# The down projection by seven products of quarters, token-major, for the first two parts of each FFN, and gate/up product blocks that share a PSUM bank

## The chip, the core and the metric

The kernel runs on one core of a Trainium2 chip. The metric is device time in microseconds of one execution. The core has TensorE (matmuls; PE in the profile, with the load of the stationary operand as a row of its own, PEld), VectorE (DVE), ScalarE (ACT), GpSimd (POOL) and SyncE (SP), which run side by side and wait for each other by semaphores. Matmuls accumulate in PSUM, which has banks of 512 float32 columns per partition; all else lies in SBUF.

## The reference

A decoder trunk of two layers (`DEPTH`) on 512 tokens and 1024 features, float32. Each layer runs a SwiGLU FFN, a mixer, a cross attention and a second FFN, so there are four FFNs, all of one form:

```
def swiglu_ffn(h, w_gu, w_down):
    gu = h @ w_gu
    gate, up = jnp.split(gu, 2, axis=-1)
    return (jax.nn.silu(gate) * up) @ w_down
...
f = swiglu_ffn(rms_norm(h, ffn1_pre_g[i]), ffn1_w_gu[i], ffn1_w_down[i])
h = h + 0.5 * rms_norm(f, ffn1_post_g[i])
```

`D_FF` is 2816, which is 22 blocks of 128 hidden features. Mixers and cross attention are the same in both kernels.

## The kernel before

Every float32 product is made from three matmuls in a reduced format: an operand is split into `hi` (a cast on ScalarE) and `lo` (the remainder, a subtraction on VectorE), and `mm3` (L77 to L81) adds hi·hi, hi·lo and lo·hi into PSUM. So each weight tile and each activation tile passes once through ScalarE (L74) and once through VectorE (L75) before TensorE can use it. `parts` does that for a raw weight tile of 512 KB, into a ring of four `whi`/`wlo` pairs (`N_W`); the raw tiles have a ring of seven (`N_R`).

An FFN works through the 22 hidden blocks in three parts of 8, 8 and 6 (`FF_PARTS`, L33). In a part it first makes the hidden features, two blocks at a time, feature-major (features on partitions, tokens along a row), by `seven` (L292): gate and up of the two blocks by seven products of quarters in place of eight, a scheme of the Strassen kind. The activations' quarters and their sums (`x.a11`, `x.a12`, `x.a22`, `x.x1` to `x.x4`) are made once per FFN in `Quarters`; the weights' sums are made from the quarters `b11`, `b21`, `b22` and the sums `t1`, `t3`, partly by DMAs that add into a raw tile (L299 and L302, on the GpSimd queue). A product is 2 x 4 x 3 = 24 matmuls with 256 columns, so a `seven` has 168. PSUM accumulators A, B and C are two banks each, one for each of the two feature blocks u, with 256 of 512 columns in use. The first two blocks of an FFN are made without the scheme (`fm_quad`). `done` applies silu and the gate product and splits the result into the `Hidden` tile of the part.

Then the part's down projection: for each half c of the 1024 output columns, four accumulators (`accs`, one for each 128 tokens), over 8 hidden blocks, `tm_part` (L334): hidden features are stationary, weights move 512 columns at a time, so 2 x 8 x 4 x 3 = 192 matmuls with 512 columns. The result is copied to `f` (ScalarE, first part) or added to it (VectorE, second part). The third part's projection is joined with the norm that follows (`tm_last`).

Which instruction comes first on an engine is decided when the kernel is built: a scheduler with a cost model of its own lays out one fixed list for each engine, and an engine works through its list in order. The SBUF pool `big` has 13 tiles of 8 KB per partition (`N_S`).

Of the kernel before, what the change touches and what calls it, by code (L numbers as in the profile page):

```python
# [4 lines left out]
F32 = mybir.dt.float32  # L5
# [30 lines left out]
def trunk_kernel(tc, x, mem, ffn1_pre_g, ffn1_w_gu, ffn1_w_down, ffn1_post_g,  # L36
# [8 lines left out]
    with ExitStack() as es:  # L45
# [194 lines left out]
        def fm_raw(w, i, c0):  # L240
            raw = raw_tile([P, 4, 256])
            nc.sync.dma_start(out=raw, in_=fm_rows(w, i, c0))
            return raw
# [26 lines left out]
        def psa():  # L270
            return pa.tile([P, 512], F32, name="psa", tag="a")
# [20 lines left out]
        def seven(w, ca, cb, x, done, mid=None):  # L292

            b21 = fm_raw(w, 1, ca)
            b11 = fm_raw(w, 0, ca)
            t1 = fm_raw(w, 0, cb)
            nc.gpsimd.dma_start(out=t1, in_=fm_rows(w, 0, ca), accum_op=ALU.add)  # L299
            b22 = fm_raw(w, 1, cb)  # L300
            t3 = fm_raw(w, 0, cb)
            nc.gpsimd.dma_start(out=t3, in_=fm_rows(w, 1, cb), accum_op=ALU.add)  # L302
            banks = {n: [psa(), psa()] for n in "BAC"}
            out_a = qt([P, 2, SEQ])
            out_b = qt([P, 2, SEQ])
            lo_h, hi_h = slice(0, HALF), slice(HALF, SEQ)

            def product(n, raw, ops, start):
                wh = parts(raw, (P, 4, 256))
                for u in range(2):  # L310
                    for k in range(4):
                        mm3(banks[n][u][:, :HALF], tuple(t_[:, k, u * P:(u + 1) * P] for t_ in wh),
                            (ops[:, 0, k], ops[:, 1, k]), start and k == 0, k == 3, False)
                return [b[:, :HALF] for b in banks[n]]

            pb = product("B", b21, x.a12, True)
            for u, p_ in enumerate(product("A", b11, x.a11, True)):
                nc.scalar.copy(out=out_a[:, u, lo_h], in_=p_)
                nc.vector.tensor_tensor(out=out_a[:, u, lo_h], in0=pb[u], in1=out_a[:, u, lo_h], op=ALU.add)
            for u, p_ in enumerate(product("C", t1, x.x1, True)):  # L320
                nc.scalar.copy(out=out_b[:, u, hi_h], in_=p_)
            nc.vector.tensor_tensor(out=t1, in0=t1, in1=b22, op=ALU.add)
            for u, p_ in enumerate(product("A", t1, x.x2, False)):
                nc.scalar.copy(out=out_b[:, u, lo_h], in_=p_)
            for u, p_ in enumerate(product("C", b22, x.x4, False)):
                nc.vector.tensor_tensor(out=out_b[:, u, lo_h], in0=p_, in1=out_b[:, u, lo_h], op=ALU.subtract)
            for u, p_ in enumerate(product("A", t3, x.x3, False)):
                nc.vector.tensor_tensor(out=out_b[:, u, hi_h], in0=out_b[:, u, hi_h], in1=p_, op=ALU.subtract)
            if mid:
                mid()  # L330
            nc.vector.tensor_tensor(out=t1, in0=t1, in1=b21, op=ALU.add)
            done(out_a, out_b, product("A", t1, x.a22, False))

        def tm_part(accs, a, w, ks, first, last, ts=range(NT)):  # L334
            for k in ks:
# [128 lines left out]
                return t[:, 0, j % 2, c0:c1], t[:, 1, j % 2, c0:c1]  # L464

        def ffn(pre, w_gu, w_down, post_g, nxt):
            f = None
            for j0, j1 in FF_PARTS:
                hid = Hidden()
                for j in range(j0, j1, 2):  # L470
                    if j == 0:
                        ws = pre.ws
                        ps = fm_quad([ws[0], ws[2], ws[1], ws[3]], pre, True)
                        s_ = qt([P, 2, SEQ])
                        for i in range(2):
                            nc.scalar.activation(out=s_[:, i, :], in_=ps[2 * i], func=AF.Silu)
                            nc.vector.tensor_tensor(out=s_[:, i, :], in0=ps[2 * i + 1], in1=s_[:, i, :],
                                                    op=ALU.mult)
                        ht = hid.put(j - j0)
                        split(ht[:, 0], ht[:, 1], s_)  # L480
                        continue

                    def done(ga, ub, last, j=j):
                        nc.scalar.activation(out=ga[:, :, :HALF], in_=ga[:, :, :HALF], func=AF.Silu)
                        for u in range(2):
                            nc.scalar.activation(out=ga[:, u, HALF:], in_=last[u], func=AF.Silu)
                        nc.vector.tensor_tensor(out=ga, in0=ga, in1=ub, op=ALU.mult)  # L487
                        ht = hid.put(j - j0)
                        split(ht[:, 0], ht[:, 1], ga)

                    wk = {}
                    mid = (lambda: last_weights(w_down, j0, j1 - j0, wk, True)) if j == NFF - 2 else None
                    seven(w_gu, j * P, FF + j * P, pre.x, done, mid)
                n = j1 - j0
                if j1 == NFF:
                    nx = nxt()
                    last_weights(w_down, j0, n, wk, False)
                    tm_last(hid, wk, n, post_g, nx, f)
                    break
                fresh = f is None  # L500
                if fresh:
                    f = [big(F32, (P, 2, D)) for _ in range(2)]
                for c in range(2):
                    accs = [psa() for _ in range(NT)]
                    for k0 in range(0, n, 4):
                        wk = dict(zip(range(k0, k0 + 4), w_tm(w_down, j0 + k0, 4, c * 512)))
                        tm_part(accs, hid, wk, range(k0, k0 + 4), 0, n - 1)
                    for t in range(NT):
                        dst = f[t // 2][:, t % 2, c * 512:(c + 1) * 512]
                        if fresh:  # L510
                            nc.scalar.copy(out=dst, in_=accs[t])
                        else:
                            nc.vector.tensor_tensor(out=dst, in0=accs[t], in1=dst, op=ALU.add)
            return nx

        spilled = {}
# [439 lines left out]
```

## Time and profile before

| | |
|---|---|
| median of three runs | 2040.62 us (2039.35 to 2043.59) |
| the profiled execution | 2044.45 us, of which its span is 2042.6 us |
| TensorE busy | 1992.6 us, 98% of the span |
| VectorE / ScalarE / GpSimd busy | 1329.9 / 991.9 / 176.3 us |
| mean granted clock of TensorE | 0.994 |
| moved by DMA | 277.96 MB |

The span reaches from the first to the last instruction of one execution; times below are microseconds from its start. In the timeline of TensorE a row's second number is the duration of one matmul, and since matmuls overlap in the array, the cost of one is the distance from its start to the next one's. A bracket at a row's end is the idle time of the engine ahead of it and what ended it.

### The profile page before, as it was taken

What the parts mean: (1) busy time and instruction counts of PE and PEld (TensorE: products, weight loads), DVE (VectorE), ACT (ScalarE), POOL (GpSimd) and SP (SyncE); (2) the same over time, 40 slices, a digit from 0 to 9 for tenths busy, and PEclk for the clock granted to TensorE, in tenths of its full rate; (3) what the DMA queues carried; (4) which work ended last, traced back from release to release, by engine and by line L of the source; (5) the groups of instructions that cost most, each with busy time, mean ns of one, the idle gap of its engine ahead of it and who ended that gap; (6) DMA issues with size and microseconds to landing.
All of it is one profiled execution on the core that took longest, in us unless ns stands there. A gap on an engine that the chain in (4) does not pass through costs nothing. (4 is left out here: it accounts for less than half of the span.)

```text
span 2042.6 us, 31836 instructions
## 1 busy us (share of the span) xinstructions
PE 1992.6 (98%) x13033; PEld 1826.1 (89%) x13033; DVE 1329.9 (65%) x1743; ACT 991.9 (49%) x1565; POOL 176.3 (9%) x181
## 2 busy tenths in 40 slices
PE   7999999998999999999999999999999999999998
PEld 7989999887878879899898989999878879999897
DVE  6737567799946458457487836657666648647475
ACT  6535345544555356445255635435545545445262
POOL 1001010121010011010001101010000000000000
PEclk9999999999999999999999999999999999999999
DMA  6747554324632235565572656646152225657561
GB/s 197 197 113 190 158 137 146 115 83 133 232 130 93 61 94 143 156 143 168 125 215 53 160 149 148 182 115 196 63 175 78 78 57 139 177 124 176 130 158 54
DMA packets 228520, 277.96 MB, mean 136 GB/s; under 512 B 8476, under 2 KB 188276, under 8 KB 227350
## 3 DMA queue, kind: packets, MB, share of 16 engines
q1 hardware_dynamic: 184806, 225.54, 34.5%
q0 software_dynamic: 43392, 50.34, 15.0%
q8 instruction: 102, 1.67, 0.3%
q14 instruction: 44, 0.36, 0.1%
q10 hardware_dynamic: 176, 0.05, 0.0%
HBM read 269.60 MB, written 6.29 MB: 135 GB/s over the span
## 5 line engine op out<-in xcount | busy, mean ns | idle before, releaser
L81 PE MATMUL psa<-big,wlo 128*128 128x256 f32 (+1 forms) x3056 | 885.8, 290 | 7.5 <-DVE wlo L75 7.5
L79 PE MATMUL psa<-big,whi 128*128 128x256 f32 (+1 forms) x3056 | 886.6, 291 | 5.1 <-ACT big L74 4.2
L80 PE MATMUL psa<-big,whi 128*128 128x256 f32 (+1 forms) x3056 | 887.0, 291 | 0.5 <-DVE big L75 0.5
L75 DVE TENSOR_TENSOR wlo<-raw,whi 128x1024 fp32r<-128x1024 f32 x474 | 580.1, 1227 | 462.7 <-ACT whi L74 461.2
L74 ACT CAST whi<-raw 128x1024 fp32r<-128x1024 f32 x474 | 495.7, 1050 | 581.0 <-PE psa L81 262.6
L81 PEld LDWEIGHTS psa<-big,wlo 128*128 128x128 f32 x3056 | 588.1, 193 | 15.9 <-DVE wlo L75 8.7
L79 PEld LDWEIGHTS psa<-big,whi 128*128 128x128 f32 x3056 | 587.7, 193 | 14.8 <-ACT big L74 6.8
L80 PEld LDWEIGHTS psa<-big,whi 128*128 128x128 f32 x3056 | 588.7, 193 | 8.6 <-DVE big L75 1.5
L79 PE MATMUL psa<-whi,big 128*128 128x512 f32 x928 | 363.9, 392 | 1.6 <-DVE big L75 1.6
L80 PE MATMUL psa<-wlo,big 128*128 128x512 f32 x928 | 362.5, 391 | 0.0
L81 PE MATMUL psa<-whi,big 128*128 128x512 f32 x928 | 362.1, 391 | 0.0
L79 PEld LDWEIGHTS psa<-whi,big 128*128 128x128 f32 x928 | 174.9, 188 | 38.1 <-DVE big L75 2.0
L81 PEld LDWEIGHTS psa<-whi,big 128*128 128x128 f32 x928 | 174.8, 188 | 36.5 <-DVE big L75 0.2
L80 PEld LDWEIGHTS psa<-wlo,big 128*128 128x128 f32 x928 | 174.8, 188 | 36.0 <-DVE wlo L75 0.6
L299 POOL DMA_DIRECT2D raw<-in_ffn_w_gu_dram x40 | 51.7, 1293 | 861.8 <-DMA raw<-in_ffn_w_gu_dram 585.3
L158 POOL TENSOR_TENSOR r<-m,nhalf 128x1 f32<-128x1 f32 x74 | 49.3, 666 | 453.5 <-DVE m L442 179.3
L302 POOL DMA_DIRECT2D raw<-in_ffn_w_gu_dram x40 | 51.5, 1286 | 401.7 <-DMA raw<-in_ffn_w_gu_dram 280.7
L645 DVE SCALAR_TENSOR_TENSOR big<-big,par 128x511 f32<-128x511 f32 (+29 forms) x120 | 85.6, 766 | 0.0
L75 DVE TENSOR_TENSOR big<-q,big 128x1024 fp32r<-128x1024 f32 x62 | 75.3, 1220 | 15.6 <-ACT big L74 15.6
L79 PE MATMUL psa<-big 128*128 128x512 f32 (+1 forms) x224 | 81.0, 363 | 0.8 <-ACT big L74 0.8
L74 ACT CAST big<-q 128x1024 fp32r<-128x1024 f32 x62 | 64.8, 1051 | 34.9 <-DVE q L487 24.9
L80 PE MATMUL psa<-big 128*128 128x512 f32 (+1 forms) x224 | 80.7, 360 | 0.0
(142 smaller groups left out, 1494.5 us busy)
## 6 DMA issues: line engine op xcount, KB each, us to landing
raw<-in_ffn_w_gu_dram SPq DMA_DIRECT2D x216, 512.0 KB, 4.6
raw<-in_ffn_w_down_dram SPq DMA_DIRECT2D x88, 512.0 KB, 4.2
raw<-in_ffn_w_gu_dram POOLq DMA_DIRECT2D x80, 512.0 KB, 6.3
raw<-in_xa_w_kv_dram SPq DMA_DIRECT2D x32, 512.0 KB, 3.7
raw<-in_ev_w_in_dram SPq DMA_DIRECT2D x16, 512.0 KB, 4.2
raw<-in_xa_w_q_dram SPq DMA_DIRECT2D x16, 512.0 KB, 4.3
raw<-in_xa_w_o_dram SPq DMA_DIRECT2D x16, 512.0 KB, 3.7
raw<-in_ev_w_out_dram SPq DMA_DIRECT2D x8, 512.0 KB, 4.9
```

What stands on the lines that cost most here:

```text
L74: nc.scalar.copy(out=hi, in_=src)
L75: nc.vector.tensor_tensor(out=lo, in0=src, in1=hi.bitcast(F32), op=ALU.subtract)
L79: nc.tensor.matmul(out=ps, lhsT=lhs[0], rhs=rhs[0], start=start, stop=skip, skip_group_check=skip)
L80: nc.tensor.matmul(out=ps, lhsT=lhs[0], rhs=rhs[1], start=False, stop=skip, skip_group_check=skip)
L81: nc.tensor.matmul(out=ps, lhsT=lhs[1], rhs=rhs[0], start=False, stop=stop or skip, skip_group_check=skip)
L158: nc.gpsimd.tensor_tensor(out=r, in0=m, in1=nhalf.broadcast_to([P, n]), op=ALU.pow)
L299: nc.gpsimd.dma_start(out=t1, in_=fm_rows(w, 0, ca), accum_op=ALU.add)
L302: nc.gpsimd.dma_start(out=t3, in_=fm_rows(w, 1, cb), accum_op=ALU.add)
L645: nc.vector.scalar_tensor_tensor(out=acc[:, c, s_:], in0=z[:, c, :SEQ - s_], scalar=par[:, c, CONV - 1 - s_:CONV - s_], in1=acc[:, c, s_:] ...
```

## The change

In `seven` the accumulators A, B and C are one bank each, with the two feature blocks side by side, so that one instruction takes both out. The products come in another order (A, B, A, C, A, C, A; before B, A, C, A, C, A, A), the sum t1+b22 goes into the tile of `b11` and is needed by the third product instead of the fourth, and silu and gate product are done for each half of the tokens apart. In the first two parts the result stays float32, in two tiles r of a part, and is not split there.

The new `seven_tm` makes the down projection of these parts by seven products as well: tokens in halves, the part's 8 hidden blocks in halves, output columns in halves. The stationary operands are quarters of r and their sums (made on VectorE, split into hi and lo); the moving ones are quarters of the weights and their sums, made by adding DMAs (`put`) and on VectorE. A product is 4 x 2 x 3 = 24 matmuls with 512 columns, so the stage has 168. Each product's result is added to `f`, or subtracted.

```diff
-            banks = {n: [psa(), psa()] for n in "BAC"}
+            banks = {n: psa().rearrange("p (u n) -> p u n", u=2) for n in "ABC"}
...
+            p1 = product("A", b11, x.a11, True)
+            nc.scalar.copy(out=out_a[:, :, lo_h], in_=p1)
+            p2 = product("B", b21, x.a12, True)
+            nc.vector.tensor_tensor(out=out_a[:, :, lo_h], in0=p2, in1=out_a[:, :, lo_h], op=add)
+            nc.vector.tensor_tensor(out=b11, in0=t1, in1=b22, op=add)
+            u2 = product("A", b11, x.x2, False)
+            nc.scalar.copy(out=out_b[:, :, lo_h], in_=u2)
+            q5 = product("C", t1, x.x1, True)
+            nc.scalar.copy(out=out_b[:, :, hi_h], in_=q5)
+            u3 = product("A", t3, x.x3, False)
+            nc.vector.tensor_tensor(out=out_b[:, :, hi_h], in0=out_b[:, :, hi_h], in1=u3, op=sub)
+            u7 = product("C", b22, x.x4, False)
+            nc.vector.tensor_tensor(out=out_b[:, :, lo_h], in0=u7, in1=out_b[:, :, lo_h], op=sub)
+            done(out_a, out_b, None)
             if mid:
                 mid()
-            nc.vector.tensor_tensor(out=t1, in0=t1, in1=b21, op=ALU.add)
-            done(out_a, out_b, product("A", t1, x.a22, False))
+            nc.vector.tensor_tensor(out=b11, in0=b11, in1=b21, op=add)
+            done(out_a, out_b, product("A", b11, x.a22, False))
+
+        def seven_tm(w, k0, r, a11, f, fresh):
...
+            t1 = load(0, 1)
+            put(t1, 0, 0)
+            b11 = load(0, 0)
+            b22 = load(1, 1)
+            b21 = load(1, 0)
+            r11, r12, r21, r22 = r[0][:, :, :HALF], r[1][:, :, :HALF], r[0][:, :, HALF:], r[1][:, :, HALF:]
...
+            def product(n, raws, ops):
+                start = n not in banks
+                if start:
+                    banks[n] = [psa(), psa()]
+                for kk in range(2):
+                    wh = parts(raws[kk], (P, 2, 512))
+                    for s_ in range(2):
+                        for i in range(2):
+                            k = 2 * kk + i
+                            cs = slice(s_ * P, (s_ + 1) * P)
+                            mm3(banks[n][s_], (ops[:, 0, k, cs], ops[:, 1, k, cs]), (wh[0][:, i], wh[1][:, i]),
+                                start and k == 0, k == 3, False)
+                return banks[n]
...
+            e = qt([P, 4, HALF])
+            nc.vector.tensor_tensor(out=e, in0=r21, in1=r22, op=sub)
+            x1 = operand(e)
+            p1 = product("A", b11, a11)
...
+            take(0, 0, p1, None if fresh else add)
+            nc.vector.tensor_tensor(out=e, in0=e, in1=r11, op=sub)
+            x2 = operand(e)
+            q5 = product("C", t1, x1)
+            for kk in range(2):
+                nc.vector.tensor_tensor(out=t1[kk], in0=t1[kk], in1=b22[kk], op=add)
...
+            take(1, 1, q5, None if fresh else add)
+            a12 = operand(r12)
+            u2 = product("A", t1, x2)
+            put(t1, 1, 0)
+            t3 = load(0, 1)
+            take(0, 1, u2, None if fresh else "from")
+            nc.vector.tensor_tensor(out=r11, in0=r11, in1=r21, op=sub)
+            x3 = operand(r11)
+            take(0, 0, product("B", b21, a12), add)
+            for kk in range(2):
+                nc.vector.tensor_tensor(out=t3[kk], in0=t3[kk], in1=b22[kk], op=add)
+            nc.vector.tensor_tensor(out=e, in0=e, in1=r12, op=add)
+            x4 = operand(e)
+            take(1, 1, product("A", t3, x3), sub)
+            a22 = operand(r22)
+            take(0, 1, product("C", b22, x4), "from")
+            take(1, 0, product("A", t1, a22), None if fresh else add)
...
-                for c in range(2):
-                    accs = [psa() for _ in range(NT)]
-                    for k0 in range(0, n, 4):
-                        wk = dict(zip(range(k0, k0 + 4), w_tm(w_down, j0 + k0, 4, c * 512)))
-                        tm_part(accs, hid, wk, range(k0, k0 + 4), 0, n - 1)
...
+                else:
+                    seven_tm(w_down, j0, r, a11, f, not f)
```

What the change does to the engines' fixed lists is shown at three places.

The first place is the passage from the last `seven` of the second part of the first FFN to its down projection, on VectorE. Before: `wlo` rows are weight tiles, `q4_2173` is the gate product, `big_2389` the lo half of the last `Hidden` tile, L513 the sums into `f`.

```order
L75 TENSOR_TENSOR wlo_2459<-raw_2456,whi_2458 128x1024
L75 TENSOR_TENSOR wlo_2465<-raw_2462,whi_2464 128x1024
L487 TENSOR_TENSOR q4_2173<-q4_2173,q4_2174 128x1024
L75 TENSOR_TENSOR big_2389<-q4_2173,big_2389 128x1024
L75 TENSOR_TENSOR wlo_2527<-raw_2524,whi_2526 128x1024
L75 TENSOR_TENSOR wlo_2533<-raw_2530,whi_2532 128x1024
L75 TENSOR_TENSOR wlo_2587<-raw_2584,whi_2586 128x1024
L513 TENSOR_TENSOR big_1186<-psa_2392,big_1186 128x512
```

After, from the same passage on: `raw_2354` and `raw_2356` are t1, `raw_2492` is t3[0], `raw_2364` and `raw_2366` are b22, `big_1449` and `big_1450` the tiles r, `q4_2372` is e, `big_2374` x1's lo half, `big_1209` and `big_1252` are `f`, L391 is `take`, `psa_2377` and `psa_2378` are the banks A, `psa_2417` one of C.

```order
L404 TENSOR_TENSOR raw_2354<-raw_2354,raw_2364 128x1024
L417 TENSOR_TENSOR raw_2492<-raw_2492,raw_2364 128x1024
L580 TENSOR_TENSOR big_1450<-q4_2144,q4_2145 128x2x256
L75 TENSOR_TENSOR wlo_2436<-raw_2356,whi_2435 128x1024
L394 TENSOR_TENSOR q4_2372<-big_1449,big_1450 128x1024
L391 TENSOR_TENSOR big_1209<-big_1209,psa_2377 128x512
L391 TENSOR_TENSOR big_1209<-big_1209,psa_2378 128x512
L75 TENSOR_TENSOR big_2374<-q4_2372,big_2374 128x1024
L404 TENSOR_TENSOR raw_2356<-raw_2356,raw_2366 128x1024
L400 TENSOR_TENSOR q4_2372<-q4_2372,big_1449 128x1024
L75 TENSOR_TENSOR wlo_2459<-raw_2354,whi_2458 128x1024
L391 TENSOR_TENSOR big_1252<-big_1252,psa_2417 128x512
```

Three kinds of rows have come in between the gate product (L580) and x1's lo half: a weight tile, the sum e, and two sums of the first product into `f`; a sum of weights (L417) stands ahead of the gate product.

The second place is the same stage further on, where the fifth and sixth products begin. On TensorE, `big_2499` is x3, `big_2541` is x4, `whi_2544`/`wlo_2545` belong to t3[0], `whi_2581` to b22[0], `psa_2417` and `psa_2418` are the banks C:

```order
L79 MATMUL psa_2377<-whi_2544,big_2499 128x512
L79 MATMUL psa_2378<-whi_2544,big_2499 128x512
L79 MATMUL psa_2417<-whi_2581,big_2541 128x512
L79 MATMUL psa_2418<-whi_2581,big_2541 128x512
L80 MATMUL psa_2377<-wlo_2545,big_2499 128x512
L81 MATMUL psa_2377<-whi_2544,big_2499 128x512
```

On VectorE, `big_2499` and `big_2541` are x3's and x4's lo halves, `raw_2494` is t3[1], `psa_2502` and `psa_2503` are the banks B:

```order
L75 TENSOR_TENSOR big_2499<-big_1449,big_2499 128x1024
L417 TENSOR_TENSOR raw_2494<-raw_2494,raw_2366 128x1024
L391 TENSOR_TENSOR big_1209<-big_1209,psa_2502 128x512
L418 TENSOR_TENSOR q4_2372<-q4_2372,big_1450 128x1024
L391 TENSOR_TENSOR big_1209<-big_1209,psa_2503 128x512
L75 TENSOR_TENSOR wlo_2545<-raw_2492,whi_2544 128x1024
L75 TENSOR_TENSOR big_2541<-q4_2372,big_2541 128x1024
```

Two matmuls of the sixth product (with x4) stand behind the first two of the fifth, and on VectorE the sum e for x4 (L418) stands behind the sum t3[1] and a `take` of B.

The third place is inside the passage from one `seven` to the next, on VectorE. Before: `raw_1681`, `raw_1683`, `raw_1685`, `raw_1688` are the next one's b21, b11, t1 and b22; L326 and L328 take out products of the current one, L322 is the sum t1+b22.

```order
L75 TENSOR_TENSOR wlo_1702<-raw_1681,whi_1701 128x1024
L326 TENSOR_TENSOR q4_1463<-psa_1460,q4_1463 128x256
L326 TENSOR_TENSOR q4_1463<-psa_1461,q4_1463 128x256
L75 TENSOR_TENSOR wlo_1730<-raw_1683,whi_1729 128x1024
L328 TENSOR_TENSOR q4_1463<-q4_1463,psa_1458 128x256
L328 TENSOR_TENSOR q4_1463<-q4_1463,psa_1459 128x256
L75 TENSOR_TENSOR wlo_1762<-raw_1685,whi_1761 128x1024
L322 TENSOR_TENSOR raw_1685<-raw_1685,raw_1688 128x1024
```

After: `raw_2129`, `raw_2131`, `raw_2133`, `raw_2136` are the next one's b11, b21, t1 and b22; L320, L327 and L329 take out products of the current one, L321 is the sum t1+b22.

```order
L75 TENSOR_TENSOR wlo_2068<-raw_1911,whi_2067 128x1024
L75 TENSOR_TENSOR wlo_2100<-raw_1904,whi_2099 128x1024
L75 TENSOR_TENSOR wlo_2147<-raw_2129,whi_2146 128x1024
L321 TENSOR_TENSOR raw_2129<-raw_2133,raw_2136 128x1024
L327 TENSOR_TENSOR q4_1920<-q4_1920,psa_1916 128x2x256
L75 TENSOR_TENSOR wlo_2176<-raw_2131,whi_2175 128x1024
L329 TENSOR_TENSOR q4_1920<-psa_1918,q4_1920 128x2x256
```

The sum stood behind the L328 rows and now stands ahead of the L327 row, which takes out u3.

## Rows read from the trace of the kernel before

**Rows 1.** The page: busy time by engine; the granted clock in 40 slices.

```profile
PE 1992.6 (98%) x13033; PEld 1826.1 (89%) x13033; DVE 1329.9 (65%) x1743; ACT 991.9 (49%) x1565; POOL 176.3 (9%) x181
PEclk9999999999999999999999999999999999999999
```

**Rows 2.** Windows: first part's down stage, second part's four sevens, its down stage.

```profile
core 0: us, PE busy (x) PEld busy (x) DVE busy (x) ACT busy (x) POOL busy (x), PEclk, DMA share, GB/s
104.00:147.60 43.60, 43.60 (x195) 36.09 (x194) 13.39 (x11) 13.68 (x17) 3.85 (x3) 1.00 0.48 115
147.60:227.80 80.20, 80.20 (x669) 80.20 (x668) 57.71 (x65) 45.18 (x68) 6.41 (x5) 1.00 0.67 173
227.80:271.40 43.60, 43.60 (x197) 36.22 (x196) 17.35 (x18) 9.77 (x10) 3.88 (x3) 1.00 0.49 115
```

**Rows 3.** Timeline of TensorE: first matmul of a down stage, and the first behind it.

```profile
104.03 0.40 PE L79 MATMUL psa<-whi,big 128*128 128x512 f32 x1
...
147.58 0.28 PE L79 MATMUL psa<-big,whi 128*128 128x256 f32 x1
...
228.37 0.40 PE L79 MATMUL psa<-whi,big 128*128 128x512 f32 x1
```

**Rows 4.** Groups by form: line, engine, operation, tiles, count, busy, mean ns, idle before.

```profile
L75 DVE TENSOR_TENSOR wlo<-raw,whi 128x1024 fp32r<-128x1024 f32 x474 | 580.1, 1227 | 462.7 <-ACT whi L74 461.2
L74 ACT CAST whi<-raw 128x1024 fp32r<-128x1024 f32 x474 | 495.7, 1050 | 581.0 <-PE psa L81 262.6 <-PE psa L80 205.4 <-issue 63.7
...
L513 DVE TENSOR_TENSOR big<-psa,big 128x512 f32<-128x512 f32 x32 | 21.5, 689 | 4.4 <-PE psa L81 4.4
...
L511 ACT COPY big<-psa 128x512 f32<-128x512 f32 x32 | 18.8, 587 | 21.0 <-PE psa L81 18.8
```

**Rows 5.** Timeline of VectorE: operations back to back, 1024 and 512 columns.

```profile
67.89 1.22 DVE L75 TENSOR_TENSOR wlo<-raw,whi 128x1024 fp32r<-128x1024 f32 x1
69.03 0.42 DVE L319 TENSOR_TENSOR q<-psa,q 128x256 f32<-128x256 f32 x1
...
270.17 2.64 DVE L513 TENSOR_TENSOR big<-psa,big 128x512 f32<-128x512 f32 x4
```

**Rows 6.** The page's DMA issues: KB of each, median us to landing.

```profile
raw<-in_ffn_w_gu_dram SPq DMA_DIRECT2D x216, 512.0 KB, 4.6
raw<-in_ffn_w_down_dram SPq DMA_DIRECT2D x88, 512.0 KB, 4.2
raw<-in_ffn_w_gu_dram POOLq DMA_DIRECT2D x80, 512.0 KB, 6.3
```

**Rows 7.** The adding DMAs of L299, from 60 to 230 us: time to landing.

```profile
DMA to landing us min/median/max: 5.9/6.0/9.1
```

**Rows 8.** Timeline of TensorE: first and last idle gap over 2 us, one between.

```profile
466.14 0.39 PE L81 MATMUL psa<-big,wlo 128*128 128x256 f32 x1 [2.75 <-DVE wlo L75]
...
1509.15 0.99 PE L79 MATMUL psa<-big,whi 128*128 128x512 f32 x2 [2.71 <-ACT big L74]
1509.93 0.63 PE L79 MATMUL psa<-whi,big 128*128 128x512 f32 x1
1510.36 0.63 PE L80 MATMUL psa<-wlo,big 128*128 128x512 f32 x1
...
1696.45 0.66 PE L182 MATMUL tps<-ident,q 128*128 128x128 f32 x4 [2.80 <-ACT q L175]
```

**Rows 9.** Windows at the gaps of rows 8: PE busy, granted clock, DMA share, GB/s.

```profile
463.00:467.00 4.00, 1.25 (x11) 1.00 0.35 116
1508.00:1512.00 4.00, 2.85 (x7) 0.68 1.05 393
1512.00:1516.00 4.00, 4.00 (x17) 0.89 0.24 85
1695.00:1699.00 4.00, 2.55 (x15) 0.77 0.48 75
```

More of the change, by code (lines that the diff above doesn't have):

```diff
@@ L292, in seven @@
         def seven(w, ca, cb, x, done, mid=None):
+            b11 = fm_raw(w, 0, ca)
             b21 = fm_raw(w, 1, ca)
-            b11 = fm_raw(w, 0, ca)
             t1 = fm_raw(w, 0, cb)
@@ L306, in seven @@
             lo_h, hi_h = slice(0, HALF), slice(HALF, SEQ)
+            sub, add = ALU.subtract, ALU.add
             def product(n, raw, ops, start):
@@ L311, in product @@
                     for k in range(4):
[L312 to L326, printed above, removed]
@@ L327, in seven @@
-            for u, p_ in enumerate(product("A", t3, x.x3, False)):
-                nc.vector.tensor_tensor(out=out_b[:, u, hi_h], in0=out_b[:, u, hi_h], in1=p_, op=ALU.subtract)
+                        mm3(banks[n][:, u, :], tuple(t_[:, k, u * P:(u + 1) * P] for t_ in wh),
+                            (ops[:, 0, k], ops[:, 1, k]), start and u == k == 0, k == 3, False)
+                return banks[n]
+            p1 = product("A", b11, x.a11, True)
+            nc.scalar.copy(out=out_a[:, :, lo_h], in_=p1)
@@ L466, in ffn @@
         def ffn(pre, w_gu, w_down, post_g, nxt):
-            f = None
+            f = []
             for j0, j1 in FF_PARTS:
+                ending = j1 == NFF
                 hid = Hidden()
+                r = None if ending else [big(F32), big(F32)]
+                a11 = None
                 for j in range(j0, j1, 2):
+                    to = None if ending else r[(j - j0) // 4][:, (j - j0) % 4:(j - j0) % 4 + 2, :]
                     if j == 0:
@@ L476, in ffn, with done @@
                             nc.scalar.activation(out=s_[:, i, :], in_=ps[2 * i], func=AF.Silu)
-                            nc.vector.tensor_tensor(out=s_[:, i, :], in0=ps[2 * i + 1], in1=s_[:, i, :],
+                            nc.vector.tensor_tensor(out=to[:, i, :], in0=ps[2 * i + 1], in1=s_[:, i, :],
                                                     op=ALU.mult)
-                        ht = hid.put(j - j0)
-                        split(ht[:, 0], ht[:, 1], s_)
                         continue
[L483 to L489, printed above, removed]
+                    def done(ga, ub, last, j=j, to=to):
+                        cs = slice(HALF, SEQ) if last is not None else slice(0, HALF)
+                        g = ga[:, :, cs]
+                        nc.scalar.activation(out=g, in_=g if last is None else last, func=AF.Silu)
+                        nc.vector.tensor_tensor(out=(ga if ending else to)[:, :, cs], in0=g, in1=ub[:, :, cs],
+                                                op=ALU.mult)
+                        if ending and last is not None:
+                            ht = hid.put(j - j0)
+                            split(ht[:, 0], ht[:, 1], ga)
                     wk = {}
@@ L493, in ffn @@
                     seven(w_gu, j * P, FF + j * P, pre.x, done, mid)
+                    if not ending and j - j0 == 2:
+                        a11 = ops4()
+                        split(a11[:, 0], a11[:, 1], r[0][:, :, :HALF])
                 n = j1 - j0
-                if j1 == NFF:
+                if ending:
                     nx = nxt()
@@ L498, in ffn @@
                     tm_last(hid, wk, n, post_g, nx, f)
[L499 to L502, printed above, removed]
-                for c in range(2):
-                    accs = [psa() for _ in range(NT)]
-                    for k0 in range(0, n, 4):
-                        wk = dict(zip(range(k0, k0 + 4), w_tm(w_down, j0 + k0, 4, c * 512)))
-                        tm_part(accs, hid, wk, range(k0, k0 + 4), 0, n - 1)
[L508 to L513, printed above, removed]
+                else:
+                    seven_tm(w_down, j0, r, a11, f, not f)
             return nx
```

31 lines of the change are left out of this document (added).

## Prediction, made before the changed kernel ran

> **What bounds the kernel now.** The page comes first: TensorE is busy 98% of the span, VectorE 65%, ScalarE 49%, and the clock row is 9 throughout [rows 1]. That is an average, so the stages that change are read next, as windows: in both down stages and in the sevens between them TensorE has no idle time at all, VectorE is busy 13.4 and 17.4 us of 43.6 in the down stages and 57.7 of 80.2 in the four sevens, and the clock is full [rows 2]. Here the time is the number of matmuls times their distance; any matmul saved is won, and any wait that TensorE gets is lost in full. The distance comes from the timeline: a down stage begins at 104.03 and the next matmul of another kind at 147.58, so 192 matmuls take 43.55 us, 0.2268 us each; from there to 228.37 lie four sevens, 28 products, 2.89 us each [rows 3].
>
> **What is removed.** A down stage has 168 matmuls instead of 192, of the same shape: 24 x 0.2268 = 5.44 us less. There are 2 parts in each of 4 FFNs, so 8 x 5.44 = 43.5 us is the most that the change can give. The Trainium skill ("TensorE: Matmul & The Clock Gate", section "Back-to-back issue gap") gives some 0.131 us for a sustained matmul of 512 columns; by that, an estimate, 192 fewer would save 25.2 us, less than the waits below cost; the trace has the distance itself, and it decides.
>
> **What is added, outside TensorE.** A pass over 1024 columns takes VectorE 1.23 us until its result is there [rows 4], and 1.14 from start to start (67.89 to 69.03) when nothing makes it wait; 512 columns take 0.69 and 2.64 / 4, some 0.65 [rows 4, 5]. ScalarE takes 1.05 for a cast, 0.59 for a copy of 512 columns [rows 4]. A new down stage gives VectorE 14 weight tiles, 6 lo halves of operands, 4 sums of activations and 4 of weights, 28 x 1.14 = 31.9 us, and takes: 14 x 0.65 = 9.1 in the second part, 6 x 0.65 = 3.9 in the first, where 8 go to ScalarE. That is 41.0 and 35.8 us beside 168 x 0.2268 = 38.1 us of matmuls, where VectorE did 17.4 and 13.4. So VectorE goes from idle to about as loaded as TensorE, and what counts is the order of its list.
>
> ScalarE's 20 casts (21.0 us, and 4.7 of copies in the first part) lie beside 38.1 us. DMAs become 10 loads and 4 adding ones for 16 loads, under a DMA share of 0.48 [rows 2]. In the sevens three take-outs of 512 columns replace six of 256, the gate product is two passes, and the Hidden split is gone in two parts of three: VectorE gets slightly less to do where it has 22 us of slack in 80 [rows 2]. A take-out now waits for both blocks u, but no bank is written by two products in a row, so it has a product's 2.89 us for 0.69. I put these at nothing; that cover gone, a seven would pay one take-out, 0.7 us.
>
> **Waits in the second part's down stage.** I walk down the list of the first two places above with these durations, time 0 being the end of the last seven (a semaphore's hop counted as 0.05, the array's drain as 0.2; both are estimates from what the durations in [rows 5, 8] exceed the distances by).
> - The last silu stands behind a cast on ScalarE and ends at 1.8. VectorE does the sum t3[0] first: its load goes out at -3.2, when the second tile of b11 is split and its place free, and lands 4.2 later [rows 6]; so VectorE is free at 2.2. Gate product until 2.85, a weight tile until 4.0, e is there at 5.2, the cast x1 at 6.3. The first product ends at 5.44: TensorE waits 0.95. Four hi matmuls follow; the lo half, behind two takes, is there at 7.7: 0.4 more. The second product ends at 12.25.
> - x2's lo half stands behind a sum, e, two weight tiles and a take that needs three quarters of the second product (11.1): ready at 14.1. TensorE has six matmuls to do in between and waits 0.55. The third product ends at 18.7, the fourth (B) at 23.7.
> - t3[1]'s load needs the place of the first tile of b21, free at 18.2; it lands at 22.5, and VectorE stands until then. Then its sum (free at 23.65), a take of B, e (25.5), a cast (26.75). On TensorE two matmuls of the sixth product want x4 right behind the first two of the fifth: it stands from 24.15 to 26.8, and 0.1 for a weight tile, 2.75 us. After that nothing is late: the end is 37.3 + 5.44.
> Together 0.95 + 0.4 + 0.55 + 2.75 = 4.65 us.
>
> **Waits in the first part's.** There the copies run on ScalarE and the sixth product is not pulled ahead. x1's lo half stands behind two weight passes more: ready at 8.65, so 0.95 + 1.4; x2's at 14.3, 0.25. Together 2.6 us; the later operands are 2 us or more ahead.
>
> **The clock.** After the first 20 us the trace has six idle gaps of TensorE over 2 us (first and last in [rows 8]). In five of them the clock then fell to 1.2 GHz, its lower level, where a 512-column matmul takes 0.43 us (1509.93 to 1510.36) [rows 8]; the windows show 0.68 and then 0.89, so 4 x 0.32 + 4 x 0.11 = 1.7 us lost; only behind the gap that ended at 466.14 did it stay at 1.00 [rows 9]. The one walked wait of that size is the 2.65 us in the second part: I count 1.6 us in each, since 0.1 of the wait behind it goes under. Bounds: nothing, and 1.7 in each of the eight.
>
> **Sum.** -43.5 + 4 x 4.65 + 4 x 2.6 + 4 x 1.6 = -43.5 + 18.6 + 10.4 + 6.4 = -8.1 us. The profiled execution took 2044.45 (span 2042.6 and 1.85 around it), so 2036.3; it lies 3.8 above the median, and against the median the forecast is 2040.6 - 8.1 = **2032.5 us**. The walked waits are the unknown: bounds are no wait at all (-43.5) and, per part, a stage as long as VectorE's whole work behind the 7.7 us that x1 takes, 48.7 against 38.1, 10.6 each (+41). I take the walk, since the list and each duration are known and only the landings vary; if every wait is 25% off, the sum moves by 7.
>
> **The rivals** (0.2%, 4 us, is what a measurement of this kernel tells from no change).
> - *No fall of the clock.* The gaps are just over those after which it fell, and one of six did not: -14.5, **2026**.
> - *Waits mostly vanish*, because silu, take-outs and landings come earlier than I count: for it speaks that before the change no wait lasted in an FFN; against it that VectorE has 41 us of work where it had 17. Half of the waits gone, and no fall of the clock: -29, **2012**; 1997 at best.
> - *The gain is eaten.* The clock falls in all eight parts, as the first part's two waits of 0.95 and 1.4 lie close together: 4 x 1.6 more, -1.7, **2039**. The same comes from 1.5 us more per second part, for which landings 1.5 us later suffice. By the Trainium skill's warning of idle gaps between matmul bursts ("TensorE: Matmul & The Clock Gate", section "Why this matters for your kernels") this is the case to fear.
> - *Slower: the sevens.* In the third place the sum t1+b22 of the next seven now stands ahead of the take-out of u3, and the last product writes u3's bank, so it waits for both. t1's load goes out when the fourth product's weights are split (2.6 us into the seven), lands 4.6 later [rows 6], is added to in 6.3 [rows 6]: 13.6. The last product begins at 6 x 2.89 = 17.3, and sum and take-out need 1.14 + 0.69 + 0.05, so the sum must start by 15.4. That is 1.8 us of slack; the longest landing there was, 9.1 [rows 7], overdraws it by 1.0. Before, a landing had until behind these take-outs. 7 sevens of an FFN are followed by another, 28 in all: 1.0 each is +28, **2060**; from 0.3 us each on the gain is gone. Against it: medians leave it hidden.
>
> **How the numbers follow.** Forecast 0.44 (its own range 2026 to 2037), no fall of the clock 0.16, waits vanish 0.10, gain eaten 0.14, sevens 0.16. The range 2010 to 2050 leaves out half of the vanishing case and half of the sevens'. Faster by over 0.2% (under 2036.5): 0.42 + 0.16 + 0.10 = 0.68. Within: 0.02 + 0.14 = 0.16. Slower: 0.16.
>
> **What would show it.** The down stages of the first FFN, 43.6 us long, should be some 40.7 (first part) and 44.3 (second, with the fall); VectorE 36 and 41 us busy in them; TensorE's waits named x1 and x2 (lo halves, `big` by VectorE) and, in the second part only, one over 2 us for `big` by ScalarE in the middle; the clock under 1.00 right behind it. In the sevens TensorE should have no wait. Wrong I am if the first of these waits is missing, if VectorE waits for L321's adding DMA while TensorE stands, or if stretches outside the FFNs move.

## The result, and the profile after

The changed kernel takes 2073.55 us in the median (2067.58 to 2076.67, four runs) where the kernel before takes 2039.98: ratio 1.016, 95% interval 1.013 to 1.019. It is slower by 33 us; the forecast was 8 faster. Its profiled span is 2074.8 us, 32.2 longer, at a mean granted clock of 0.984 (before 0.994).

The page of the kernel after, to compare with [rows 1] and [rows 6]:

```profile
PE 1973.7 (95%) x12841; PEld 1800.8 (87%) x12841; DVE 1502.3 (72%) x1847; ACT 1036.5 (50%) x1477; POOL 214.3 (10%) x213
PEclk9999999999999999999999999999999999999999
...
raw<-in_ffn_w_gu_dram POOLq DMA_DIRECT2D x80, 512.0 KB, 8.3
raw<-in_ffn_w_down_dram POOLq DMA_DIRECT2D x32, 512.0 KB, 6.7
```

The 192 matmuls are gone (13033 to 12841), and TensorE still loses: it is busy 95% of a longer span. The adding DMAs of the gate/up weights land in 8.3 us instead of 6.3.

Windows of the kernel after: the first part's down stage, the second part's sevens, its down stage (as [rows 2]):

```profile
111.40:152.60 41.20, 38.99 (x170) 31.35 (x170) 37.84 (x37) 24.53 (x28) 4.95 (x4) 1.00 0.64 153
152.60:232.60 80.00, 80.00 (x668) 79.96 (x668) 55.15 (x55) 40.46 (x49) 10.11 (x8) 1.00 0.80 197
233.20:275.00 41.80, 39.42 (x172) 31.16 (x170) 39.31 (x41) 19.82 (x20) 4.95 (x4) 1.00 0.54 132
```

TensorE's first matmuls of these stretches and of the one behind (as [rows 3]):

```profile
111.45 0.40 PE L79 MATMUL psa<-whi,big 128*128 128x512 f32 x1
...
152.65 0.28 PE L79 MATMUL psa<-big,whi 128*128 128x256 f32 x1
...
233.28 0.40 PE L79 MATMUL psa<-whi,big 128*128 128x512 f32 x1
```

These stretches have become shorter: down stages of 41.2 and 41.7 us where 43.55 stood, sevens of 80.6 where 80.8 stood. From the first 512-column matmul of a down stage to the first of 256 behind it, the eight stages take 332.8 us together (before 348.4): they gain 15.6. But the first down stage begins at 111.45, not at 104.03 [rows 3]. The loss lies ahead of it, in the sevens of the first part, and likewise in those of the third.

What TensorE waits for, after (line waited for: us in total, times, longest):

```profile
PE psa L79 <- DVE q L327: 22.3, 8, 5.1
PE psa L79 <- ACT big L74: 17.8, 21, 2.7
PE psa L79 <- ACT q L318: 12.9, 7, 3.0
...
PE psa L81 <- DVE big L75: 4.5, 4, 1.1
```

L327 takes out u3 (it reads the product from its PSUM bank), L318 copies the first product p1: both belong to `seven`, and together they make 35.2 us in 15 waits that the kernel before did not have. By place, 22.9 us of them lie in the first parts, 0.5 in the second and 11.8 in the third. The two other rows are the down stage's operands (part of the first stood before the change too).

Two of these waits on TensorE, in the first part of the first FFN:

```profile
67.61 0.28 PE L81 MATMUL psa<-big,wlo 128*128 128x256 f32 x1
70.76 0.58 PE L79 MATMUL psa<-big,whi 128*128 128x256 f32 x1 [2.87 <-ACT q L318]
71.14 0.41 PE L80 MATMUL psa<-big,whi 128*128 128x256 f32 x1
71.35 0.41 PE L81 MATMUL psa<-big,wlo 128*128 128x256 f32 x1
...
83.60 0.28 PE L81 MATMUL psa<-big,wlo 128*128 128x256 f32 x1
86.82 0.39 PE L79 MATMUL psa<-big,whi 128*128 128x256 f32 x1 [2.93 <-DVE q L327]
```

Behind the first, after one distance of 0.38 us, two matmuls lie 0.21 us apart instead of 0.12, as at 1.2 GHz; the granted clock is 0.88 in the window from 66 to 80 us. It fell behind the second too: 0.72 from 86 to 92. What stands behind both waits is on VectorE:

```profile
57.41 1.23 DVE L75 TENSOR_TENSOR wlo<-raw,whi 128x1024 fp32r<-128x1024 f32 x1
64.21 1.23 DVE L321 TENSOR_TENSOR raw<-raw 128x1024 f32<-128x1024 f32 x1 [5.57 <-DMA raw<-in_ffn_w_gu_dram]
...
79.17 1.23 DVE L75 TENSOR_TENSOR wlo<-raw,whi 128x1024 fp32r<-128x1024 f32 x1 [1.64 <-ACT whi L74]
84.94 1.23 DVE L321 TENSOR_TENSOR raw<-raw 128x1024 f32<-128x1024 f32 x1 [4.55 <-DMA raw<-in_ffn_w_gu_dram]
86.08 0.68 DVE L327 TENSOR_TENSOR q<-q,psa 128x512 f32<-128x512 f32 x1
```

VectorE stands for t1's adding DMA with the sum t1+b22 (L321) at the head of its list, and u3's take-out, long due, is behind it. ScalarE's list shows the other wait:

```profile
56.34 1.05 ACT L74 CAST whi<-raw 128x1024 fp32r<-128x1024 f32 x1 [0.72 <-ACT whi L74]
65.55 1.05 ACT L74 CAST whi<-raw 128x1024 fp32r<-128x1024 f32 x1 [8.16 <-DVE raw L321]
...
68.24 1.98 ACT L74 CAST whi<-raw 128x1024 fp32r<-128x1024 f32 x2
70.12 0.58 ACT L318 COPY q<-psa 128x512 f32<-128x512 f32 x1
```

The cast of the same sum keeps ScalarE idle for 8.16 us; p1's copy, for which the bank of the third product waits, is five operations behind it. When t1's load went out is on SyncE's and GpSimd's lists:

```profile
70.87 0.37 SPq L242 DMA_DIRECT2D raw<-in_ffn_w_gu_dram  x1
...
74.88 1.28 POOL L299 DMA_DIRECT2D raw<-in_ffn_w_gu_dram  x1 [14.88 <-DVE wlo L75]
```

Load at 70.87, adding DMA at 74.88, sum at 84.94: 10.06 us from issue to use.

### The profile page after: what moved, and what is told of

It reads as the page before. It is cut to its first block, busy times and chain, and to the rows that moved or that the text cites. A ratio compares the mean times of both kernels' runs of the same rounds, so it can differ in the third digit from the quotient of the medians.

```text
span 2074.8 us, 31706 instructions
## 1 busy us (share of the span) xinstructions
PE 1973.7 (95%) x12841; PEld 1800.8 (87%) x12841; DVE 1502.3 (72%) x1847; ACT 1036.5 (50%) x1477; POOL 214.3 (10%) x213
## 5 line engine op out<-in xcount | busy, mean ns | idle before, releaser
L74 ACT CAST whi<-raw 128x1024 fp32r<-128x1024 f32 x522 | 544.8, 1050 | 668.3 <-PE psa L80 256.3
L75 DVE TENSOR_TENSOR wlo<-raw,whi 128x1024 fp32r<-128x1024 f32 x522 | 636.3, 1224 | 256.6 <-ACT whi L74 255.0
L79 PE MATMUL psa<-whi,big 128*128 128x512 f32 x864 | 338.5, 394 | 14.4 <-ACT big L74 12.8
L81 PE MATMUL psa<-whi,big 128*128 128x512 f32 x864 | 336.0, 392 | 5.1 <-DVE big L75 4.5
L80 PE MATMUL psa<-wlo,big 128*128 128x512 f32 x864 | 337.7, 391 | 0.0
L79 PEld LDWEIGHTS psa<-whi,big 128*128 128x128 f32 x864 | 162.0, 188 | 53.6 <-ACT big L74 20.3
L81 PEld LDWEIGHTS psa<-whi,big 128*128 128x128 f32 x864 | 162.7, 188 | 44.5 <-DVE big L75 11.2
L299 POOL DMA_DIRECT2D raw<-in_ffn_w_gu_dram x40 | 51.7, 1292 | 788.8 <-DMA raw<-in_ffn_w_gu_dram 438.6
L321 DVE TENSOR_TENSOR raw<-raw 128x1024 f32<-128x1024 f32 x40 | 48.9, 1223 | 70.3 <-DMA raw<-in_ffn_w_gu_dram 58.6
L79 PE MATMUL psa<-big 128*128 128x512 f32 (+1 forms) x224 | 80.9, 363 | 0.8 <-ACT big L74 0.8
L80 PE MATMUL psa<-big 128*128 128x512 f32 (+1 forms) x224 | 80.8, 361 | 0.0
L81 PE MATMUL psa<-big 128*128 128x512 f32 (+1 forms) x224 | 80.2, 359 | 0.0
L75 DVE TENSOR_TENSOR big<-big 128x512 fp32r<-128x512 f32 (+1 forms) x70 | 66.0, 946 | 8.8 <-ACT big L74 8.3
```

The costliest lines, as they stand in the source:

```text
L321: nc.vector.tensor_tensor(out=b11, in0=t1, in1=b22, op=add)
```

## The experiments

Theory 1: the new order in `seven` makes t1's adding DMA late, and two engines' lists stand for it. Theory 2: it is the shared banks, whose take-outs wait for both blocks u. Theory 3: it is the new down stage, which through the raw ring and its DMAs upsets the sevens behind it.

**The halves apart.** The changed seven with the old down projection:

```diff
-                    seven_tm(w_down, j0, r, a11, f, not f)
...
+                for c in range(2):
+                    accs = [psa() for _ in range(NT)]
...
+                        tm_part(accs, hid, wk, range(k0, k0 + 4), 0, n - 1)
```

> The changed seven alone (product order, shared banks, two gate passes) with the old down projection. Theory 1 (the new order of the sevens makes them wait for t1's adding DMA and for ScalarE's list): 2040 plus some 35 us of waits in the sevens plus 15 to 20 us at half clock behind them, so 2085 to 2095, with gaps of 2 to 5 us in the first part's and third part's sevens. Theory 2 (shared banks: a take-out that waits for both blocks): the same sign, but small and even, 0.3 to 0.7 us in every seven, 2050 to 2060. Theory 3 (the new down stage upsets the sevens behind it through the raw ring and its adding DMAs): no change, 2040 within 4.

The new down projection with the old seven:

```diff
-            banks = {n: psa().rearrange("p (u n) -> p u n", u=2) for n in "ABC"}
+            banks = {n: [psa(), psa()] for n in "BAC"}
...
-            p1 = product("A", b11, x.a11, True)
...
+            pb = product("B", b21, x.a12, True)
```

> The new down projection alone, with the old seven (its order, two banks for each accumulator, sums into t1). Theory 1: -43.5 of matmuls, +20 of walked waits in the down stages, +3 to +6 at half clock, so 2017 to 2025, and no gap over 1 us in the sevens. Theory 2: the same. Theory 3: the sevens' gaps stay and it is no faster than before, 2045 to 2075.

Measured: seven alone 2063.5 us (ratio 1.011, 1.010 to 1.013), down alone 2030.4 (0.995, 0.994 to 0.996). TensorE's waits of the first, then of the second:

```profile
PE psa L79 <- ACT q L318: 13.7, 4, 4.1
```

```profile
PE psa L79 <- ACT big L74: 19.6, 21, 2.7
...
PE psa L81 <- DVE big L75: 4.5, 4, 1.1
```

The loss is the seven's, and beside the old seven the down projection is a gain of 10 us. Theory 3 as it was put falls. But both halves of theory 1 were off: 23 us lost where 45 to 55 were expected, 10 gained where 15 to 23 were. The parts sum to +12.7, the whole is +33: some 20 us come only from both together. TensorE's waits for L318 and L327 show where: 13.9 us with the seven alone, all in the first parts, and 35.2 with both, 22.9 in the first parts and 11.8 in the third. For the third parts the traces show how. GpSimd's issue of t1's adding DMA for the first seven of the third part, old down stage and then new one:

```profile
243.22 1.28 POOL L299 DMA_DIRECT2D raw<-in_ffn_w_gu_dram  x1 [33.20 <-DMA raw<-in_ffn_w_gu_dram]
```

```profile
266.26 1.28 POOL L299 DMA_DIRECT2D raw<-in_ffn_w_gu_dram  x1 [18.62 <-ACT whi L74]
```

The sums that need them start at 265.79 and 274.44: with the old down stage the adding DMA is issued 22.6 us ahead of its sum, with the new one 8.2, and in the sevens behind it waits appear that the half without it does not have (L327: none over 0.4 us in that kernel). So in the third parts the new down stage amplifies the loss; that is read from the two traces, and no run isolates it. The 9 us more in the first parts can't come this way, since no new down stage lies ahead of them in the FFN. There t1's adding DMA of the third seven of the first FFN takes 9.98 us with both and 7.59 with the seven alone, beside other loads of the down weights; why is open.

**t1 first**, as in the diff, in the changed kernel, and the same with the old down projection:

```diff
+            t1 = fm_raw(w, 0, cb)
+            nc.gpsimd.dma_start(out=t1, in_=fm_rows(w, 0, ca), accum_op=ALU.add)
             b11 = fm_raw(w, 0, ca)
             b21 = fm_raw(w, 1, ca)
-            t1 = fm_raw(w, 0, cb)
-            nc.gpsimd.dma_start(out=t1, in_=fm_rows(w, 0, ca), accum_op=ALU.add)
```

> The changed kernel with one move: in seven, t1's load and its adding DMA are issued first, ahead of b11 and b21. Theory 1: the adding DMA gets some 3 us or more of lead, the sevens' waits and the falls of the clock behind them go, so 2073.5 - 35 - 15 = 2023, 2018 to 2035. Theory 2: unchanged, 2070 to 2077. Theory 3: unchanged or some us less, 2060 to 2077.

> The changed seven alone with the old down projection, and t1's load and adding DMA issued first. Theory 1: its four waits on the copy of the first product (13.7 us) and the half clock behind them go: 2040 within 5. If it stays at 2055 or over, the waits of the sevens do not come from t1 being late. Theory 2: 2050 to 2060.

Measured 2024.6 (0.992, 0.990 to 0.993) and 2037.1 (0.998, 0.997 to 0.999). The same place of the program in the kernel with t1 first and all else changed (the adding DMA is L297 here):

```profile
61.99 1.28 POOL L297 DMA_DIRECT2D raw<-in_ffn_w_gu_dram  x1 [0.72 <-DVE raw L321]
```

```profile
77.82 1.23 DVE L321 TENSOR_TENSOR raw<-raw 128x1024 f32<-128x1024 f32 x1
78.97 0.68 DVE L327 TENSOR_TENSOR q<-q,psa 128x512 f32<-128x512 f32 x1
```

15.8 us from issue to use instead of 10.06, and VectorE doesn't stand. It is the lead that has grown: over the whole kernel t1's adding DMAs still take 7.8 us in the median (8.3 in the changed kernel, 6.1 before). The waits for L318 and L327 are gone from both kernels. Against the changed kernel the span is 48.5 us shorter. Outside the eight down stages TensorE stands 35.8 us less, and its busy time is 18.8 us less: matmuls that had run at half clock behind the waits. The down stages themselves take 6.1 us more than in the changed kernel (338.9), as the clock now falls in the first parts.

**t1 second**, behind b11:

```diff
             b11 = fm_raw(w, 0, ca)
-            b21 = fm_raw(w, 1, ca)
             t1 = fm_raw(w, 0, cb)
             nc.gpsimd.dma_start(out=t1, in_=fm_rows(w, 0, ca), accum_op=ALU.add)
+            b21 = fm_raw(w, 1, ca)
```

> The changed kernel with t1's load and adding DMA issued second, behind b11 and ahead of b21: half the lead of the kernel with t1 first. Theory 1: between 2024.6 (t1 first) and 2073.5 (t1 third), and since a load goes out 1.1 us and more earlier against waits of 2 to 5 us, nearer the first: 2030 to 2050, with some waits on take-outs left in the first and third parts. If it is at 2024 too, the lead needed is under one place of the queue; if at 2070, the place does not matter and what t1 first changed was something else.

Measured 2024.7 (0.992): as with t1 first. The expectation of a half effect missed, for a reason that the queue shows. t1's load (third seven of the first FFN) goes out at 57.33 us, one of five in a row:

```profile
57.33 0.37 SPq L242 DMA_DIRECT2D raw<-in_ffn_w_gu_dram  x1
```

In the changed kernel it goes out at 70.87, right behind the split of the t1 before it, which ends at 70.85 and frees a slot of the raw ring. The load now lies 23.8 us ahead of the last product of the seven before (which begins at 81.11), and not 12.85. So the lead follows from when a slot comes free, and one place in the queue decides which slot t1 gets; that is read from the times of the loads.

**One adding DMA less**: t3 summed on VectorE in `seven`.

```diff
-            nc.gpsimd.dma_start(out=t3, in_=fm_rows(w, 1, cb), accum_op=ALU.add)
+            nc.vector.tensor_tensor(out=t3, in0=t3, in1=b22, op=ALU.add)
```

> The changed kernel with t3 = b12 + b22 made on VectorE (one pass of 1.14 us per seven) instead of by an adding DMA, so that t1's adding DMA is the only one of a seven. Theory 1, if what makes t1 late is that two adding DMAs now run side by side: t1's lands in some 6 us as before the change instead of 10, most waits in the sevens go, 2030 to 2045. Theory 1, if t1 is late because its load goes out late: 8 us or more to landing stay or do not matter, 2065 to 2080. Theories 2 and 3: no change beyond a few us.

Measured 2080.4 (1.020, 1.018 to 1.021). TensorE's waits, and t1's adding DMAs from 45 to 110 us:

```profile
PE psa L79 <- DVE q L327: 35.2, 13, 5.8
...
PE psa L79 <- ACT q L318: 4.1, 5, 1.4
```

```profile
DMA to landing us min/median/max: 9.5/9.6/9.7
```

The one issued at 53.81 has no other adding DMA beside it and takes 9.7 us: that two of them slow each other falls as the reason. With t1 first the opposite can be seen: the one issued at 61.99 has t3's beside it (59.98 to 65.97), but no plain load of these weights goes out between 57.34 and 67.08, and it takes 6.7 us. The waits for the two lines are 39.3 us (before this edit 35.2) and move from the copy to the take-out; t3's sum, a further operation of VectorE that stands for a load (71.1 us of idle time ahead of it), is the likely reason, not a shown one.

**Old order, shared banks.** The changed kernel with products, loads and sums in the old order, t1+b22 into t1's tile, one bank per accumulator:

```diff
+            p2 = product("B", b21, x.a12, True)
             p1 = product("A", b11, x.a11, True)
             nc.scalar.copy(out=out_a[:, :, lo_h], in_=p1)
-            p2 = product("B", b21, x.a12, True)
...
+            nc.vector.tensor_tensor(out=t1, in0=t1, in1=b22, op=add)
+            u2 = product("A", t1, x.x2, False)
```

> The changed kernel with the old order of products, loads and sums in seven (B, A, C, A, C, A, A; t1+b22 into t1's own tile), but still one bank for each accumulator. Theory 1 (the order is what makes the sevens wait): like the new down projection beside the whole old seven, 2030 within 6, no wait on the copy of the first product and few on take-outs. Theory 2 (sharing a bank costs, since a take-out waits for both blocks): half or more of the 43 us between that kernel and the changed one stays, 2050 to 2075.

Measured 2039.8 (0.999, 0.998 to 1.000), between the two expectations. No wait for a take-out or for p1's copy is in its list of waits, nor in the two kernels with t1 first, which share banks too: theory 2 falls. By the medians this kernel is 9.5 us behind the down projection beside the old seven; the two profiled executions are 15.0 apart, and 7.8 of these lie in the down stages, where TensorE reaches x1 too early:

```profile
108.10 0.39 PE L81 MATMUL psa<-whi,big 128*128 128x512 f32 x1
110.62 0.50 PE L79 MATMUL psa<-whi,big 128*128 128x512 f32 x1 [2.13 <-ACT big L74]
```

It stands 2.13 us in all eight, and in six of them the clock falls behind it. The stages take 336.6 us, to which four matmuls each (0.9 us) come that are issued inside the last seven: some 344, where the other kernel's take 336.1. These four bring TensorE to x1 0.9 us sooner, and on VectorE a sum of weights (L404) stands ahead of the sum e for x1; some 5 of the 7.8 us are matmuls at half clock. The other 7 us lie outside the down stages, mostly as busy time. So this run clears the shared banks of the sevens' waits, but not of every cost.

**A better down stage.** The kernel with t1 first, and B with a12, which needs no sum, in second place (b21 is loaded ahead of b22 for it):

```diff
+            a12 = operand(r12)
             p1 = product("A", b11, a11)
...
+            take(0, 0, product("B", b21, a12), add)
...
-            a12 = operand(r12)
...
-            take(0, 0, product("B", b21, a12), add)
```

> The changed kernel with t1 first in seven (2024.6 measured) and, in the down projection, the product B with a12, which needs no sum of activations, in second place instead of fourth, so that x1 and x2 have a product's time more. If the waits of the down stages are the walked ones (x1's hi and lo, x2), some 2.1 us in each first part and 1.2 in each second go: -13, 2012, 2008 to 2018; the wait for x4 of 1.5 to 2 us stays. If they come from VectorE's load as a whole, they move to another operand and the time stays, 2020 to 2028.

And t3 by an adding DMA on top of that:

```diff
             t3 = load(0, 1)
+            put(t3, 1, 1)
...
-            for kk in range(2):
-                nc.vector.tensor_tensor(out=t3[kk], in0=t3[kk], in1=b22[kk], op=add)
```

> As the kernel with B second, and t3 in the down projection made by an adding DMA instead of VectorE, so that VectorE no longer stands for t3's load in front of x1 and x4. If that stand is what makes x4 late, another 1.5 to 2 us in each second part go, 2002 to 2012. If adding DMAs that lie close together are what hurts, as 16 more of them would then, the sevens behind the down stages get waits again and it is slower than the one without, by 5 us or more.

> The kernel with B second and t3 by an adding DMA once more, for a profile of an undisturbed execution. 1999 within 4. In its down stages of the first FFN TensorE should stand under 1 us in the first part and under 1 us in the second, where the kernel with t3 on VectorE stood 0.9 and 4.2, and few stretches should be at half clock.

B second gives 2023.4 (0.991, 0.990 to 0.993), hardly less than 2024.6. The first parts' stages fall to some 39.4 us (157.8 for four, 169.6 with t1 first alone), but the second parts' rise to 175.9 from 169.3. The wait has moved on, to a take-out (L389, `take` out of bank A) and to x4, as the second theory of that run had it:

```profile
247.80 0.50 PE L79 MATMUL psa<-whi,big 128*128 128x512 f32 x1 [0.93 <-DVE big L389]
250.01 0.80 PE L79 MATMUL psa<-whi,big 128*128 128x512 f32 x1 [1.71 <-ACT big L74]
```

With t3 off VectorE the time falls below the expected 2002 to 2012: 1998.9 us (0.979, 0.978 to 0.980), and 1999.2 (0.980, 0.979 to 0.981) in a second run, from which the profile is. Its first part's down stage and its second part's:

```profile
104.00:142.30 38.30, 38.30 (x171) 31.55 (x170) 35.63 (x35) 23.82 (x27) 8.65 (x7) 1.00 0.89 197
...
222.80:262.00 39.20, 38.72 (x171) 31.48 (x170) 38.29 (x40) 19.97 (x20) 7.90 (x7) 1.00 0.80 181
```

TensorE hardly stands any more, the mean clock is 0.997, and the eight stages take 309.4 us, 39.0 of the possible 43.5 below before. This kernel is 2% faster than the one before the change and 3.6% faster than the changed one.

**t1 third again**, beside this better down stage:

```diff
-            t1 = fm_raw(w, 0, cb)
-            nc.gpsimd.dma_start(out=t1, in_=fm_rows(w, 0, ca), accum_op=ALU.add)
             b11 = fm_raw(w, 0, ca)
             b21 = fm_raw(w, 1, ca)
+            t1 = fm_raw(w, 0, cb)
+            nc.gpsimd.dma_start(out=t1, in_=fm_rows(w, 0, ca), accum_op=ALU.add)
```

> The down projection with B second and t3 by an adding DMA, beside the changed seven with t1 in its third place again. Theory 1: the sevens' waits and the half clock behind them come back, some 49 us as between the changed kernel and the one with t1 first: 2048, 2035 to 2060. Theory 3 (the new down stage is what upsets the sevens): the better down stage would take a good part of them away, below 2030.

Measured 2054.2 (1.007, 1.006 to 1.009), 55 us worse, with the waits back and the eight down stages as before the edit (309.5 us):

```profile
PE psa L79 <- DVE q L327: 25.8, 12, 4.3
...
PE psa L79 <- ACT q L318: 10.4, 7, 2.4
```

All medians in one table (us):

| seven | old down | new down | B second, t3 by DMA |
|---|---|---|---|
| old | 2040 | 2030.4 | |
| changed | 2063.5 | 2073.6 | 2054.2 |
| changed, t1 first | 2037.1 | 2024.6 | 1999 |

Theory 1 stands: in each column t1's place decides, by 26, 49 and 55 us. With t1 first the two halves of the change nearly add up (-3.5 and -10.2, together -16.0), so the 20 us that come from both together hang on t1's place too; a down stage with few waits of its own doesn't take them away. Each edit makes the scheduler lay out all lists anew, so no run moves t1 alone; three columns with the same sign speak against another cause.

## Why the prediction was wrong

- **The matmuls.** 24 x 0.2268 in each stage: right. In the best kernel a stage of 168 takes 38.23 us, 0.2276 each. By the 0.131 us of the Trainium skill ("TensorE: Matmul & The Clock Gate", section "Back-to-back issue gap") it would be 22, an estimate; the trace disagrees, as before.
- **The down stages' waits.** The mechanism was right, the size too dear in the second parts: I expected 40.7 and 44.3 us, measured are 41.2 and 41.7 in the first FFN. All eight take 332.8 us where the forecast adds up to 340: they gain 15.6, not 8.1. The new down projection beside the old seven gives -10.2 us, near my -8.1. VectorE is busy 37.8 and 39.3 us (forecast 36 and 41). TensorE stood for x1's hi (0.65 to 1.01 us) and lo (1.13) in the first part and for x1, x2 and x4 in the second, as named, x4 for 1.37 to 1.82 us and not 2.65. (In the walk the third product's end, 18.7, is a slip: 12.25 + 0.55 + 5.44 is 18.24, and the fourth's end is counted from that.)
- **The clock in them.** The falls that I counted in each second part came in one of four (43.8 us, where the others take 41.7 to 41.8). The rival without falls took its gaps for longer than those behind which the clock had fallen; in the trace before these are 2.01 to 2.80 us, and 2.65 lies among them. In the changed kernel the clock fell mostly in the sevens.
- **The sevens: here the step failed.** "I put these at nothing": the sum has no term for the sevens. The runs show 35.2 us of waits there and some 19 us of matmuls at half clock behind them. The rival of the sevens, from medians, left 1.8 us of slack, and by the longest landing lacked 1.0. For the wait at 83.60 the terms can be read off. The load went out 12.85 us before the last product was due (83.72 - 70.87), not 17.3 - 2.6 = 14.7, since TensorE and VectorE had been late in this seven already. It and the adding DMA took 4.0 + 10.06 us, not 4.6 + 6.3. Sum and take-out took 1.88, as forecast. 14.06 + 1.88 - 12.85 = 3.1 late, which is the gap. So the rival had the place and the chain right and was under-sized: the median of [rows 6] mixes all sevens, and [rows 7] had shown 9.1 already. Lateness also breeds lateness, since the next t1's slot comes free only behind the split of this one (70.85, and the load at 70.87, 8.9 us into the seven and not 2.6).
- **What I did not see at all**: ScalarE's list. I followed the sum on VectorE to the take-out of u3, and not its cast on ScalarE, in front of p1's copy; that is 12.9 of the 35.2 us.
- **The gain eaten by the clock.** Half-clock matmuls behind the sevens' waits cost some 19 us (18.8 against t1 first, outside the down stages). The mean clock is 0.984 with these gaps, 0.997 in the kernel that has lost them and those of the down stages. I had feared it at the wrong place. The Trainium skill warns of idle gaps between matmul bursts ("TensorE: Matmul & The Clock Gate", section "Why this matters for your kernels"). The trace agrees in kind, but the warning is of longer gaps than most of these: the clock fell behind 2.87 and 2.93 us in the first part and behind 1.91 at 294.82.
- **My sign for wrong**, VectorE waiting for L321's DMA while TensorE stands, is what the trace shows (4.55 us ahead of 84.94).

## What to carry to other kernels

When a change moves an operand's use ahead, price its DMA chain at the worst landing that the trace shows near that place, from the moment at which its buffer comes free, and then go down the list of every engine that touches the operand: what matters is what stands behind the waiting instruction. A buffer's slot can give more lead than a place in the queue: here one place earlier moved the load 13.5 us ahead, 10.9 of them against the product that waits for it. In a stage of products, begin with those whose operands need no sums, and keep off the loaded engine whatever waits for a load.

## What was not expected of the hardware

- An adding DMA of 512 KB takes from 5.5 us to 10.5 in the changed kernel, with the same bytes each time. In the first FFN's first part t1's take 10.0 there, 9.5 and 9.7 with t3's sum on VectorE, and one takes 6.7 with t1 first. The slow ones have plain loads that go out 1.1 us apart just ahead and behind, and the one of 6.7 us has another adding DMA beside it and no such load from 57.34 to 67.08; that the plain loads do it was not tested.
- Two waits in the first part's down stage, 0.65 and some 1.13 us in three of the four (the first is 1.01 us in the first FFN, and 1.55 with t1 first), leave the clock alone in the changed kernel (40.8 to 41.2 us in all four). In the kernel with t1 first it fell behind them in all four (42.1 to 43.2; granted clock 0.96 over the first), and with t1 second, where all four have 0.65 and 1.13, in one (42.3, the others 40.85). What decides is open.
